# Latent features drawn between the blocks of a feed-forward, keys and values ahead of queries, and query loads on ScalarE's queue

## The chip, the cores and the metric

The kernel runs on one core of a Trainium2 chip. The metric is the device time of one execution in microseconds (us). TensorE (PE in the profile) does matmuls and transposes, VectorE (DVE) and ScalarE (ACT) read its results out of PSUM, GpSimd (POOL) does small vector work, and SyncE (SP) has a queue that starts DMAs. ScalarE has such a queue too: a DMA that it starts stands in its program among its own instructions. Each engine works through its instructions in their order.

## The reference, cut to what matters

Two layers over 1024 latent tokens and 256 context tokens of width 1024, all in float32. The first mixes with a short convolution and a gating unit, the second with attention; each ends in a feed-forward. The change touches the end of the first layer (the context's feed-forward) and the attention of the second.

```python
h_lat = _modulate(x, m_lat[0], m_lat[1]); h_ctx = _modulate(ctx, m_ctx[0], m_ctx[1])
q_l = _axial_rope(_proj_q(h_lat, w_q, q_g), tables)       # 8 heads of 128
k_l, v_l = _proj_kv(h_lat, w_kv, k_g)                     # 2 key and value heads
k_l = _axial_rope(k_l, tables)
k_c, v_c = _proj_kv(h_ctx, w_kv, k_g)                     # context: no rotation
k_all = jnp.concatenate([k_l, k_c], axis=1)
v_all = jnp.concatenate([v_l, v_c], axis=1)
y_lat = _attend(q_l, k_all, v_all) @ w_out                # softmax over 1280 keys
x = _post_norm(x, y_lat, m_lat[2], ln_g[l, 0], ln_b[l, 0])
```

`_proj_q` and `_proj_kv` multiply by the weights and normalise each head by its root mean square; `_modulate` is `h * (1 + scale) + shift`.

## The kernel before

Float32 products are made of three matmuls in a rounded format: each operand is split into a rounded half (hi) and a rest (lo), and `mm3` (lines 89 to 92) multiplies hi by hi, hi by lo and lo by hi. So each operand costs one ScalarE cast and one VectorE subtraction: `split` (L201, L202) for activations, `prep` for weights (load L80, cast L84, subtraction L86).

The latent tokens are eight tiles of 128 rows, in two groups g of four. `ln_spill` normalises a tile and stores it in `xn2_d`. `ln_mod` then makes the features of a group: in eight steps k, four 128x128 transposes on TensorE (L258), two ScalarE activations with scale and shift (L192, L195) and one VectorE subtraction (L198). The context has two tiles, so its steps have two transposes and 256 columns. The transposes go through PSUM buffers of the tag `tr`, of which there are two.

In the kernel before, this part of the program reads: spill and features of group 0, spill and features of group 1; the context's feed-forward `ffn` in blocks of two hidden tiles (weights prepared, gate and up products of 256 columns, SiLU at L470, products with the output weights); normalisation and features of the context; q projections (half 0, then half 1 of the heads, eight tiles each); keys and values of the context; keys and values of the latent groups 0 and 1. `tok_mm` makes a projected tile in 24 matmuls, `rms_rope` (L900 to L922) normalises and rotates it over ScalarE, VectorE and GpSimd, and transposes (L944 for q, L969 and L981 for keys) turn it. Queries of tiles 4 to 7 are stored in DRAM (`q_d`).

The attention goes through units of a tile, a key head and a pair of heads. `load_q` fetches `q_d` for tiles 4 to 7, two loads of 256 KB for each tile and key head, 16 in all. They are not let ahead of the normalisation (`norm`, L1041, GpSimd) of an earlier unit. The scores of a unit begin two units ahead of its use; the first matmuls that read a loaded q tile are those on the context's keys. `resid_bg` and `resid_store` load, scale and store the residual in the background (L1096, L1099, L1106), also on SyncE's queue.

A scheduler sets the order of instructions on each engine from its own model of time, within the data's dependences and the few ordering hints in the code.

Of the kernel before, what the change touches and what calls it, by code (L numbers as in the profile page):

```python
# [8 lines left out]
F32 = mybir.dt.float32  # L9
# [19 lines left out]
def hybrid_kernel(ctx: ExitStack, tc: tile.TileContext, A, out):  # L29
# [18 lines left out]
    def U(shape, dt):  # L48
        return up.tile(shape, dt, tag="u", name="u")
# [28 lines left out]
    def prep(src, gate=None, lo_eng=None):  # L78
        wf = wp.tile([P, 1024], F32, tag="wf", name="wf", bufs=WB[0])
        nc.sync.dma_start(out=wf, in_=src)  # L80
        if gate is not None:
            nc.vector.tensor_tensor(out=wf, in0=wf, in1=gate, op=ALU.mult)
        hi = wp.tile([P, 1024], F32R, tag="hi", name="hi", bufs=WB[1])
        nc.scalar.copy(hi, wf)  # L84
        lo = wp.tile([P, 1024], F32R, tag="lo", name="lo", bufs=WB[1])
        (lo_eng or nc.vector).tensor_tensor(out=lo, in0=wf, in1=hi.bitcast(F32), op=ALU.subtract)  # L86
        return hi, lo
# [74 lines left out]
    def step(n=1):  # L162
        for _ in range(n):
            next(bg)
# [7 lines left out]
    def mod_cols(v, l, sub, ln):  # L172
        sh, s1 = cols(v, l, 3 * sub), cols(v, l, 3 * sub + 1)
        g, b = lnc[:, ln[0], ln[1], 0, :], lnc[:, ln[0], ln[1], 1, :]
        s = const.tile([P, KD], F32, name=f"ms{v}{l}{sub}")
        o = const.tile([P, KD], F32, name=f"mo{v}{l}{sub}")
        nc.vector.tensor_scalar(out=s1, in0=s1, scalar1=1.0, scalar2=None, op0=ALU.add)
        nc.vector.tensor_tensor(out=s, in0=s1, in1=g, op=ALU.mult)
        nc.vector.tensor_tensor(out=o, in0=s1, in1=b, op=ALU.mult)
        nc.vector.tensor_tensor(out=o, in0=o, in1=sh, op=ALU.add)  # L180
        return s, o
# [18 lines left out]
    def split(src, hi, lo):  # L200
        nc.scalar.copy(hi, src)  # L201
        return nc.vector.tensor_tensor(out=lo, in0=src, in1=hi.bitcast(F32), op=ALU.subtract)  # L202
# [45 lines left out]
        while deferred:  # L248
            deferred.pop(0)()

    def ln_mod(pp, acc, so):

        n = len(acc) * P
        res = []
        for k in range(KD):
            ps = pp.tile([P, 512], F32, tag="tr", name="tr", bufs=2)
            for i, a in enumerate(acc):
                nc.tensor.transpose(ps[:, i * P:(i + 1) * P], a[k // 4][:, (k % 4) * P:(k % 4 + 1) * P], ident)  # L258
            if n == 512:
                hi, lo = U([P, 512], F32R), U([P, 512], F32R)  # L260
            else:
                t = U([P, 2, n], F32R)
                hi, lo = t[:, 0, :], t[:, 1, :]
            split_mod(ps[:, :n], so[0][:, k:k + 1], so[1][:, k:k + 1], hi, lo, True)
            res.append((hi, lo))
        return res

    def out_block(pp, acts, ws, acc, groups, xres=None, xscale=1.0):  # L270
# [184 lines left out]
        return last  # L455


    def ffn(pp, l, hT, v, acc, nb=2, steps=0, hook=None):
        groups = list(range(len(hT)))
        n = hT[0][0][0].shape[-1]  # L460
        gate = gate_bc(v, l, 5)

        def block_in(b):
            acts = {g: [] for g in groups}
            wg = [(prep(A["ffn_in"][l, j]), prep(A["ffn_in"][l, NJ + j])) for j in range(b * nb, b * nb + nb)]
            for g in groups:
                for w in wg:
                    pg = in_tile(pp, w[0], hT, g)
                    sg = T()
                    nc.scalar.activation(sg[:, :n], pg, AF.Silu)  # L470
                    pu = in_tile(pp, w[1], hT, g)
                    nc.vector.tensor_tensor(out=sg[:, :n], in0=pu, in1=sg[:, :n], op=ALU.mult)
                    hi, lo = act_pair(n)
                    marks["in"] = split(sg[:, :n], hi, lo)
                    acts[g].append((hi, lo))
            return acts

        pend = {g: [] for g in groups}
        j0 = 0

        def out(n):
            nonlocal pend, j0
            ws = [prep(A["ffn_out"][l, j0 + q], gate) for q in range(n)]
            out_block(pp, {g: pend[g][:n] for g in groups}, ws, acc, groups)
            pend = {g: pend[g][n:] for g in groups}
            j0 += n

        nblk = NJ // nb
        for b in range(nblk):
            cur = block_in(b)  # L490
            run_deferred()
            if b == nblk - 1:
                out(2 * nb - LASTK)
            elif b > 0:
                out(nb)
            pend = {g: pend[g] + cur[g] for g in groups}
            step(steps)
        if hook is not None:
            hook()
        out(LASTK)  # L500
# [218 lines left out]
    def ln_spill(a, t, xn):  # L719
        ln_norm(a)  # L720
        for h in range(2):
            nc.sync.dma_start(out=xn[t * P:(t + 1) * P, h * 512:(h + 1) * 512], in_=a[h])
# [144 lines left out]
    so = mod_cols(0, 1, 0, (0, 1))  # L867
    xr_d = dp.tile([SEQ, D], F32, name="xr_d")
    xn2_d = dp.tile([SEQ, D], F32, name="xn2_d")
    hT = []  # L870
    for g in range(2):
        for t in range(4 * g, 4 * g + 4):
            ln_spill(acc[t], t, xn2_d)
        hT.append(ln_mod(pp, [acc[t] for t in range(4 * g, 4 * g + 4)], so))


    hc = hcf
    ffn(pp, 0, hc, 1, accc)
    so = mod_cols(1, 1, 0, (0, 1))
    for t in range(2):  # L880
        ln_norm(accc[t])
    hc = [ln_mod(pp, [accc[0], accc[1]], so)]


    gqk = M2([P, 4, P])
# [2 lines left out]
    def tables(w, g):  # L888
        C, S = U([P, 4, P], F32), U([P, 4, P], F32)
        nc.sync.dma_start(out=C, in_=A["cosT"][:, 4 * g:4 * g + 4, :])  # L890
        nc.sync.dma_start(out=S, in_=A["sinT"][:, 4 * g:4 * g + 4, :])
        nc.gpsimd.tensor_tensor(out=C, in0=C, in1=gqk[:, 2 * w:2 * w + 1, :].to_broadcast([P, 4, P]), op=ALU.mult)
        nc.gpsimd.tensor_tensor(out=S, in0=S, in1=gqk[:, 2 * w + 1:2 * w + 2, :].to_broadcast([P, 4, P]), op=ALU.mult)
        return C, S
# [35 lines left out]
            mm3(ps, (a[0][:, c:c + P], a[1][:, c:c + P]), (ww[0][:, ks], ww[1][:, ks]), k == 0, k == KD - 1)  # L930
        return ps

    q_d = dp.tile([8, 2, 2, P, 512], F32, name="q_d")
    qT = {}
    qtab = [tables(0, 0), tables(0, 1)]
    for half in range(2):
        wq = [prep(A["wq"][half, i]) for i in range(4)]
        for t in range(8):
            g, i = divmod(t, 4)
            ps = tok_mm(hT[g], i * P, wq)  # L940
            q = rms_rope(ps, 4, qtab[g], i)
            tr = pp.tile([P, 512], F32, tag="tr", name="tr", bufs=2)
            for h in range(4):
                nc.tensor.transpose(tr[:, h * P:(h + 1) * P], q[:, h * P:(h + 1) * P], ident)  # L944
            hi, lo = U([P, 512], F32R), U([P, 512], F32R)
            split(tr, hi, lo)
            if g == 0:
                qT[t, half] = (hi, lo)
            else:
                nc.sync.dma_start(out=q_d[t, half, 0], in_=hi.bitcast(F32))  # L950
                nc.sync.dma_start(out=q_d[t, half, 1], in_=lo.bitcast(F32))

    wkv = [prep(A["wkv"][i]) for i in range(4)]
    kT, V = {}, []

    def kv_tile(hTg, c, tab, i):
        ps = tok_mm(hTg, c, wkv)
# [2 lines left out]
        split(ps[:, 256:512], v[:, 0, :], v[:, 1, :])  # L960
        return k, v

    Vc = []
    ktr = [pp.tile([P, 512], F32, tag="tr", name="tr", bufs=2) for _ in range(2)]
    for t in range(2):
        k, v = kv_tile(hc[0], t * P, None, 0)
        Vc.append(v)
        for kv in range(2):
            nc.tensor.transpose(ktr[kv][:, t * P:(t + 1) * P], k[:, kv * P:(kv + 1) * P], ident)  # L969
    for kv in range(2):  # L970
        c = U([P, 2, 256], F32R)
        split(ktr[kv][:, 0:256], c[:, 0, :], c[:, 1, :])
        kT[kv, 2] = (c[:, 0, :], c[:, 1, :])
    for g in range(2):
        ktab = tables(1, g)
        ktr = [pp.tile([P, 512], F32, tag="tr", name="tr", bufs=2) for _ in range(2)]
        for i in range(4):
            k, v = kv_tile(hT[g], i * P, ktab, i)
            V.append(v)
            for kv in range(2):  # L980
                nc.tensor.transpose(ktr[kv][:, i * P:(i + 1) * P], k[:, kv * P:(kv + 1) * P], ident)  # L981
        for kv in range(2):
            hi, lo = U([P, 512], F32R), U([P, 512], F32R)
            split(ktr[kv], hi, lo)
            kT[kv, g] = (hi, lo)
    V += Vc
    ppA.__exit__(None, None, None)
    wpA.__exit__(None, None, None)
# [14 lines left out]
    def load_q(n):  # L1003
        t, kv, p = units[n]
        if t >= 4 and p == 0:
            qT[t, kv] = (U([P, 512], F32R), U([P, 512], F32R))
            for x in range(2):
                i1 = nc.sync.dma_start(out=qT[t, kv][x].bitcast(F32), in_=q_d[t, kv, x])
                after(i1, [norm[2 * (n - 6)]])

    def score_a(n, h):
# [239 lines left out]
```

## Time and profile before

| | |
|---|---|
| median of 3 runs | 2629.03 us (2627.96 to 2629.47) |
| profiled execution | 2629.6 us, of which the span 2627.7 us |
| mean granted TensorE clock | 0.987 |
| busy: TensorE, VectorE, ScalarE, GpSimd | 97%, 70%, 36%, 12% |
| context's feed-forward | some 1137 to 1353 us |
| projections q, then keys and values | some 1353 to 1506 us |
| attention | some 1506 to 1834 us |

The span is the time from the first to the last instruction of the profiled execution. TensorE is the busiest engine by far. The page gives busy time over the whole span, and its chain of waits says which engine's work ended last; a timeline lists one engine's instructions in order of time with the idle time ahead of each and what ended it.

### The profile page before, as it was taken

The numbers are of one execution on the slowest core, as the hardware profiler recorded it, in microseconds if no ns is written. First come the engines' busy times: TensorE is split into PE (matmuls) and PEld (weight loads), VectorE is DVE, ScalarE is ACT, GpSimd is POOL, SyncE is SP. The second block draws the span as 40 slices with busy tenths as digits, with TensorE's granted clock in tenths as the row PEclk, the third lists the DMA queues.
The fourth block names the chain that finished last, engine by engine and source line by source line (L and its number), as shares of the span: only waits on it lengthen the run. The fifth ranks groups of instructions, "written<-read, shape, count | busy, mean of one in ns | idle before, by whom it ended". The sixth has DMA issues, their size and how long they took to land. (4 is left out here: it accounts for less than half of the span.)

```text
span 2627.7 us, 34744 instructions
## 1 busy us (share of the span) xinstructions
PE 2541.2 (97%) x12956; PEld 2138.1 (81%) x12956; DVE 1851.3 (70%) x3162; ACT 933.4 (36%) x1656; POOL 326.2 (12%) x254
## 2 busy tenths in 40 slices
PE   8999999999999999989999999999989999999997
PEld 6778888787788888879988789888868888888885
DVE  3888488999866655687759488777688665663267
ACT  1311145323233323164433277666163333342220
POOL 0132000112200020010006332222001000000001
PEclk9999999999999999989999999999999999999998
DMA  8453155344422753266541100113324222243232
GB/s 242 144 186 110 57 168 171 118 160 141 129 81 83 268 175 110 91 227 195 183 141 52 41 29 25 65 41 102 131 73 144 81 81 89 80 168 133 68 117 77
DMA packets 156106, 313.68 MB, mean 119 GB/s; under 512 B 25696, under 2 KB 45152, under 8 KB 155936
## 3 DMA queue, kind: packets, MB, share of 16 engines
q1 hardware_dynamic: 155936, 311.46, 36.1%
q8 instruction: 102, 1.67, 0.3%
q14 instruction: 68, 0.56, 0.1%
HBM read 262.05 MB, written 49.35 MB: 119 GB/s over the span
## 5 line engine op out<-in xcount | busy, mean ns | idle before, releaser
L90 PE MATMUL mm<-u,w 128*128 128x512 f32 x1232 | 480.6, 392 | 11.9 <-DVE m L591 4.5
L91 PE MATMUL mm<-u,w 128*128 128x512 f32 x1232 | 482.8, 392 | 3.8 <-DVE u L202 2.8
L92 PE MATMUL mm<-u,w 128*128 128x512 f32 x1232 | 476.7, 391 | 1.9 <-DVE w L202 1.9
L90 PE MATMUL mm<-w,u 128*128 128x512 f32 x832 | 322.7, 392 | 5.8 <-ACT u L201 3.0
L91 PE MATMUL mm<-w,u 128*128 128x512 f32 x832 | 324.3, 390 | 0.0
L92 PE MATMUL mm<-w,u 128*128 128x512 f32 x832 | 321.5, 390 | 0.0
L201 ACT CAST w<-sw 128x512 fp32r<-128x512 f32 x264 | 163.2, 622 | 419.7 <-PE mm L91 365.9
L202 DVE TENSOR_TENSOR w<-sw,w 128x512 fp32r<-128x512 f32 x264 | 191.1, 728 | 169.8 <-ACT w L201 138.5
L90 PEld LDWEIGHTS mm<-u,w 128*128 128x128 f32 x1232 | 232.8, 189 | 64.0 <-DVE m L591 6.4
L91 PEld LDWEIGHTS mm<-u,w 128*128 128x128 f32 x1232 | 232.7, 189 | 53.6 <-DVE u L202 4.6
L92 PEld LDWEIGHTS mm<-u,w 128*128 128x128 f32 x1232 | 232.8, 189 | 50.9 <-DVE w L202 2.6
L90 PE MATMUL mm<-u,hi 128*128 128x256 f32 (+1 forms) x736 | 238.5, 324 | 3.3 <-ACT tt L470 1.8
L84 ACT CAST hi<-wf 128x1024 fp32r<-128x1024 f32 x134 | 138.8, 1050 | 285.3 <-PE mm L91 76.9
L92 PE MATMUL mm<-u,lo 128*128 128x256 f32 (+1 forms) x736 | 237.5, 324 | 0.8 <-DVE lo L86 0.8
L91 PE MATMUL mm<-u,hi 128*128 128x256 f32 (+1 forms) x736 | 237.8, 323 | 0.0
L90 PE MATMUL mm<-hi,u 128*128 128x512 f32 x536 | 209.3, 395 | 3.6 <-DVE tt L917 1.3
L91 PE MATMUL mm<-lo,u 128*128 128x512 f32 x536 | 210.0, 392 | 2.1 <-DVE lo L86 2.1
L92 PE MATMUL mm<-hi,u 128*128 128x512 f32 x536 | 205.7, 393 | 0.0
L86 DVE TENSOR_TENSOR lo<-wf,hi 128x1024 fp32r<-128x1024 f32 x134 | 164.5, 1238 | 43.2 <-ACT hi L84 43.2
L90 PEld LDWEIGHTS mm<-w,u 128*128 128x128 f32 x832 | 157.2, 189 | 39.4 <-ACT u L201 3.9
L92 PEld LDWEIGHTS mm<-w,u 128*128 128x128 f32 x832 | 156.6, 188 | 32.7
L91 PEld LDWEIGHTS mm<-w,u 128*128 128x128 f32 x832 | 156.6, 188 | 32.3
(186 smaller groups left out, 4538.8 us busy)
## 6 DMA issues: line engine op xcount, KB each, us to landing
raw<-in_ffn_in SPq DMA_DIRECT2D x88, 512.0 KB
ad<-in_ada_w SPq DMA_DIRECT2D x112, 256.0 KB
act<-m SPq DMA_DIRECT2D x88, 256.0 KB
raw<-act SPq DMA_DIRECT2D x44, 512.0 KB
sw<-in_ffn_out SPq DMA_DIRECT2D x88, 256.0 KB
wf<-in_ffn_in SPq DMA_DIRECT2D x44, 512.0 KB
wf<-in_w_m SPq DMA_DIRECT2D x32, 512.0 KB
ab<-in_ada_w SPq DMA_DIRECT2D x48, 256.0 KB
```

The lines of the kernel that those rows point to most:

```text
L84: nc.scalar.copy(hi, wf)
L86: (lo_eng or nc.vector).tensor_tensor(out=lo, in0=wf, in1=hi.bitcast(F32), op=ALU.subtract)
L90: nc.tensor.matmul(ps, s[0], m[0], start=first, stop=False, skip_group_check=more)
L91: nc.tensor.matmul(ps, s[0], m[1], start=False, stop=False, skip_group_check=more)
L92: return nc.tensor.matmul(ps, s[1], m[0], start=False, stop=last, skip_group_check=more)
L201: nc.scalar.copy(hi, src)
L202: return nc.vector.tensor_tensor(out=lo, in0=src, in1=hi.bitcast(F32), op=ALU.subtract)
```

## The change

Three things change.

1. All eight latent tiles are spilled first. `ln_mod` becomes a generator, `ln_mod_k`, which stops after each of its steps; `ffn` gets an argument `each`, called at the end of every block, and takes two steps of the latent features there. Sixteen steps are thus asked for in blocks 0 to 7.
2. After the feed-forward the order is: keys and values of latent group 0, features of the context, keys and values of the context, those of latent group 1, then queries in the order (group 1, half 0), (group 1, half 1), (group 0, half 1), (group 0, half 0). The weights of half 0 are prepared twice, those of half 1 once.
3. The loads of q tiles are started from ScalarE's queue.

```diff
-    def ln_mod(pp, acc, so):
+    def ln_mod_k(pp, acc, so, res):
...
             split_mod(ps[:, :n], so[0][:, k:k + 1], so[1][:, k:k + 1], hi, lo, True)
             res.append((hi, lo))
+            yield
+
+    def ln_mod(pp, acc, so):
+        res = []
+        for _ in ln_mod_k(pp, acc, so, res):
+            pass
         return res
...
             step(steps)
+            if each is not None:
+                each(b)
...
-        hT.append(ln_mod(pp, [acc[t] for t in range(4 * g, 4 * g + 4)], so))
-    hc = hcf
-    ffn(pp, 0, hc, 1, accc)
+    for t in range(8):
+        ln_spill(acc[t], t, xn2_d)
+    def next_features(b):
+        for _ in range(2):
+            next(feats, None)
+    ffn(pp, 0, hcf, 1, accc, each=next_features)
+    for _ in feats:
+        pass
...
-    for half in range(2):
-        wq = [prep(A["wq"][half, i]) for i in range(4)]
-        for t in range(8):
...
+    kv_latent(0)
+    hc = [ln_mod(pp, [accc[0], accc[1]], soc)]
+    kv_context()
+    kv_latent(1)
...
+    for g, half in ((1, 0), (1, 1), (0, 1), (0, 0)):
+        if (g, half) in ((1, 0), (0, 1)):
+            qtab = tables(0, g)
+        if (g, half) != (0, 1):
+            wq = [prep(A["wq"][half, i]) for i in range(4)]
+        for i in range(4):
+            t = 4 * g + i
...
-                i1 = nc.sync.dma_start(out=qT[t, kv][x].bitcast(F32), in_=q_d[t, kv, x])
+                i1 = nc.scalar.dma_start(out=qT[t, kv][x].bitcast(F32), in_=q_d[t, kv, x])
                 after(i1, [norm[2 * (n - 6)]])
```

`kv_latent`, `kv_context` and the body of the query loop are the code of before, put into functions. In the changed file L257 is the feature transpose, L965 the latent keys' transpose, L1031 the q load.

The first place is the start of the context's feed-forward on TensorE; `tr<-ident,u` are feature transposes, `mm<-u,hi` and `mm<-u,lo` the first products. Before:

```order
L92 MATMUL mm<-w_9094,u 128x512
L258 MATMUL tr<-ident,u 128x128 x20
L90 MATMUL mm<-u,hi 128x256
L91 MATMUL mm<-u,hi 128x256
L92 MATMUL mm<-u,lo 128x256
L90 MATMUL mm<-u,hi 128x256
```

After:

```order
L92 MATMUL mm<-w_9094,u 128x512
L257 MATMUL tr<-ident,u 128x128 x8
L90 MATMUL mm<-u,hi 128x256
L91 MATMUL mm<-u,hi 128x256
L90 MATMUL mm<-u,hi 128x256
L91 MATMUL mm<-u,hi 128x256
L92 MATMUL mm<-u,lo 128x256
```

Twelve of the twenty transposes that stood ahead of the first product are gone from there, and the first two matmuls of a second product come ahead of the third of the first. The other transposes follow in eights between later blocks.

The second place is TensorE where the context's features are made; `tr_11864` and `tr_11872` before, `tr_12086` and `tr_12094` after, are their transposes of steps 0 and 1 (from `u_9272` and `u_9276`, the context's tiles), `mm_12065` before is a q product, `mm_12033` after the last product of `kv_latent(0)`, and `tr_11896`, `tr_11897` the keys' transposes. Before:

```order
L92 MATMUL mm_12065<-hi_11945,u_9586 128x512
L90 MATMUL mm_12065<-hi_11945,u_9596 128x512
L258 MATMUL tr_11864<-ident_75,u_9272 128x128
L258 MATMUL tr_11872<-ident_75,u_9272 128x128
L91 MATMUL mm_12065<-lo_11947,u_9596 128x512
L92 MATMUL mm_12065<-hi_11945,u_9597 128x512
L258 MATMUL tr_11864<-ident_75,u_9276 128x128
L258 MATMUL tr_11872<-ident_75,u_9276 128x128
L90 MATMUL mm_12065<-hi_11951,u_9607 128x512
```

After:

```order
L91 MATMUL mm_12033<-lo_11888,u_10418 128x512
L92 MATMUL mm_12033<-hi_11886,u_10419 128x512
L965 MATMUL tr_11896<-ident_75,tt_12020 128x128
L965 MATMUL tr_11897<-ident_75,tt_12020 128x128
L965 MATMUL tr_11896<-ident_75,tt_12065 128x128
L965 MATMUL tr_11897<-ident_75,tt_12065 128x128
L257 MATMUL tr_12086<-ident_75,u_9272 128x128
L257 MATMUL tr_12086<-ident_75,u_9276 128x128
L257 MATMUL tr_12094<-ident_75,u_9272 128x128
L257 MATMUL tr_12094<-ident_75,u_9276 128x128
L90 MATMUL mm_12152<-hi_11868,u_12089 128x512
```

Before, they lie between matmuls of a product already under way. Now they follow the transposes of the last two key tiles, with no matmul between, and the matmuls behind them (`mm_12152`, keys of the context) read their result.

The third place is the first load of a q tile: on SyncE before, where L1106 is the residual's store and L1096 its load:

```order
L1106 DMA xr_d_9526<-tt_14830 128x512
L1096 DMA tt_15063<-xn2_d_9527 128x512
L1106 DMA xr_d_9526<-tt_15063 128x512
L1008 DMA u_15256<-q_d_11930 128x512
L1008 DMA u_15257<-q_d_11930 128x512
L1096 DMA tt_15305<-xn2_d_9527 128x512
```

and on ScalarE after, where `ph` and `u` are casts of probabilities and of a unit's output:

```order
L201 CAST ph_15276<-tr_15271 128x512
L201 CAST u_15166<-tr_15190 128x256
L1031 DMA u_15280<-q_d_12434 128x512
L1031 DMA u_15281<-q_d_12434 128x512
L201 CAST ph_15307<-tr_15302 128x512
L201 CAST ph_15339<-tr_15334 128x512
```

TensorE after, with the last matmuls of that output (`tr_15190`) and the first that read the loaded `u_15280`:

```order
L90 MATMUL tr_15190<-ph_15257,u_12227 128x256
L91 MATMUL tr_15190<-u_15258,u_12227 128x256
L92 MATMUL tr_15190<-ph_15257,u_12227 128x256
L90 MATMUL tr_15286<-u_12232,u_15280 128x256
L91 MATMUL tr_15286<-u_12232,u_15280 128x256
L90 MATMUL sa_15285<-u_12078,u_15280 128x512
```

The loads have left SyncE's stores and now stand behind the cast of `tr_15190`, whose last matmul is the one just ahead of the first use. The same holds at four of the eight pairs; at two the instruction ahead is an exponential, at two a cast of probabilities (`ph`). The order of TensorE's rows here is that of before.

## Rows read from the trace of the kernel before

**Rows 1.** The page's first part: busy time, share of the span, instructions.
```profile
PE 2541.2 (97%) x12956; PEld 2138.1 (81%) x12956; DVE 1851.3 (70%) x3162; ACT 933.4 (36%) x1656; POOL 326.2 (12%) x254
```

**Rows 2.** Windows: length; PE, PEld, DVE, ACT, POOL busy (instructions); granted clock; DMA share; GB/s.
```profile
1138.00:1150.00 12.00, 8.40 (x52) 7.49 (x53) 9.72 (x16) 10.66 (x15) 1.47 (x2) 0.86 0.98 329
1166.00:1182.00 16.00, 9.63 (x50) 8.56 (x49) 14.63 (x22) 12.07 (x21) 0.00 (x0) 0.68 0.48 170
...
1200.00:1350.00 150.00, 150.00 (x1027) 140.01 (x1026) 118.31 (x146) 65.19 (x86) 0.00 (x0) 1.00 0.58 186
1385.00:1500.00 115.00, 115.00 (x546) 94.79 (x545) 80.11 (x213) 30.04 (x56) 55.21 (x51) 1.00 0.14 51
```

**Rows 3.** Timeline of TensorE, feed-forward's start: start, length, instructions [idle before <-releaser].
```profile
1136.84 1.04 PE L258 MATMUL tr<-ident,u 128*128 128x128 f32 x8
...
1167.53 0.65 PE L258 MATMUL tr<-ident,u 128*128 128x128 f32 x4 [1.25 <-ACT tt L195]
...
1175.06 0.58 PE L90 MATMUL mm<-u,hi 128*128 128x256 f32 x1 [1.84 <-ACT tt L470]
```

**Rows 4.** Timeline of ScalarE, the first two weight casts of the feed-forward.
```profile
1141.70 1.05 ACT L84 CAST hi<-wf 128x1024 fp32r<-128x1024 f32 x1
...
1144.09 1.04 ACT L84 CAST hi<-wf 128x1024 fp32r<-128x1024 f32 x1
```

**Rows 5.** Timeline of TensorE, the two waits in the projections.
```profile
1383.39 0.47 PE L90 MATMUL mm<-hi,u 128*128 128x512 f32 x1 [1.32 <-DVE tt L917]
...
1505.54 0.69 PE L981 MATMUL tr<-ident,tt 128*128 128x128 f32 x2 [3.10 <-DVE tt L922]
```

**Rows 6.** Groups by shape in the projections, GpSimd and VectorE: busy, mean ns.
```profile
L919 POOL TENSOR_TENSOR tt<-tt 128x512 f32<-128x512 f32 x16 | 22.4, 1402 | 4.4 <-DVE tt L917 2.1 <-ACT tt L900 1.3 <-PE tr L944 1.0
...
L919 POOL TENSOR_TENSOR tt<-tt 128x256 f32<-128x256 f32 x8 | 5.9, 738 | 3.1 <-DVE ms L903 3.1
...
L922 DVE TENSOR_TENSOR tt<-tt,rs 128x512 f32<-128x512 f32 x16 | 10.9, 683 | 5.5 <-POOL tt L919 5.5
...
L922 DVE TENSOR_TENSOR tt<-tt,rs 128x256 f32<-128x256 f32 x10 | 4.8, 476 | 2.5 <-POOL tt L919 1.4 <-POOL rs L905 0.9
```

**Rows 7.** Timeline of TensorE in the attention, four first uses of q tiles.
```profile
1650.02 0.28 PE L90 MATMUL tr<-u 128*128 128x256 f32 x1
...
1691.19 0.28 PE L90 MATMUL tr<-u 128*128 128x256 f32 x1
...
1711.05 0.28 PE L90 MATMUL tr<-u 128*128 128x256 f32 x1
...
1733.71 0.36 PE L90 MATMUL tr<-u 128*128 128x256 f32 x1 [3.40 <-DMA u<-q_d]
```

**Rows 8.** Windows in the attention and at its end, columns as in rows 2.
```profile
1640.00:1800.00 160.00, 149.63 (x1040) 135.51 (x1039) 122.25 (x263) 105.67 (x247) 42.15 (x31) 0.99 0.18 60
...
1734.30:1737.50 3.20, 3.20 (x16) 3.00 (x15) 0.69 (x1) 0.59 (x1) 0.00 (x0) 0.50 0.08 26
1756.00:1760.00 4.00, 3.72 (x25) 3.35 (x26) 0.88 (x3) 1.27 (x3) 1.34 (x1) 1.00 0.26 97
1833.30:1839.90 6.60, 5.78 (x13) 4.46 (x14) 6.14 (x10) 3.42 (x6) 0.00 (x0) 0.50 0.80 262
```

**Rows 9.** Timeline of ScalarE around three of these first uses.
```profile
1650.55 0.38 ACT L201 CAST u<-tr 128x256 fp32r<-128x256 f32 x1
...
1689.13 1.06 ACT L201 CAST ph<-tr 128x512 fp32r<-128x512 f32 x2
...
1711.05 0.52 ACT L1033 ACTIVATE pt<-pt,nm 128x256 f32<-128x256 f32 x1
```

**Rows 10.** Timeline of SyncE's queue, the pair of loads that came latest.
```profile
1730.95 0.88 SPq L1008 DMA_DIRECT2D u<-q_d  x2
```

**Rows 11.** Waits of SyncE's queue from 1600 to 1800: us in total, times, longest.
```profile
SPq L1106 <- DVE rc L1040: 89.7, 5, 20.3
```

**Rows 12.** Who waited for the q loads of line 1008: us, times.
```profile
  PE tr L90: 4.8, 2
```

More of the change, by code (lines that the diff above doesn't have):

```diff
@@ L249, in run_deferred @@
             deferred.pop(0)()
-    def ln_mod(pp, acc, so):
+    def ln_mod_k(pp, acc, so, res):
         n = len(acc) * P
-        res = []
         for k in range(KD):
@@ L455, in mixer, with ffn @@
         return last
-    def ffn(pp, l, hT, v, acc, nb=2, steps=0, hook=None):
+    def ffn(pp, l, hT, v, acc, nb=2, steps=0, hook=None, each=None):
         groups = list(range(len(hT)))
@@ L869, in hybrid_kernel, with to_features @@
     xn2_d = dp.tile([SEQ, D], F32, name="xn2_d")
[L870 to L873, printed above, removed]
-        hT.append(ln_mod(pp, [acc[t] for t in range(4 * g, 4 * g + 4)], so))
-    hc = hcf
-    ffn(pp, 0, hc, 1, accc)
-    so = mod_cols(1, 1, 0, (0, 1))
+    hT = [[], []]
+    def to_features():
+        for g in range(2):
+            yield from ln_mod_k(pp, [acc[t] for t in range(4 * g, 4 * g + 4)], so, hT[g])
+    feats = to_features()
+    for t in range(8):
[6 more added lines that the diff above has]
+        pass
+    soc = mod_cols(1, 1, 0, (0, 1))
     for t in range(2):
         ln_norm(accc[t])
-    hc = [ln_mod(pp, [accc[0], accc[1]], so)]
+    hc = [[]]
     gqk = M2([P, 4, P])
@@ L931, in tok_mm @@
         return ps
-    q_d = dp.tile([8, 2, 2, P, 512], F32, name="q_d")
-    qT = {}
-    qtab = [tables(0, 0), tables(0, 1)]
-    for half in range(2):
-        wq = [prep(A["wq"][half, i]) for i in range(4)]
-        for t in range(8):
[L939 to L951, printed above, removed]
     wkv = [prep(A["wkv"][i]) for i in range(4)]
-    kT, V = {}, []
+    kT, V, Vc = {}, [], []
     def kv_tile(hTg, c, tab, i):
@@ L961, in kv_tile, with kv_latent @@
         return k, v
[L963 to L974, printed above, removed]
+    def kv_latent(g):
         ktab = tables(1, g)
@@ L985, in hybrid_kernel, with kv_context @@
             kT[kv, g] = (hi, lo)
+    def kv_context():
+        ktr = [pp.tile([P, 512], F32, tag="tr", name="tr", bufs=2) for _ in range(2)]
+        for t in range(2):
+            k, v = kv_tile(hc[0], t * P, None, 0)
+            Vc.append(v)
+            for kv in range(2):
+                nc.tensor.transpose(ktr[kv][:, t * P:(t + 1) * P], k[:, kv * P:(kv + 1) * P], ident)
+        for kv in range(2):
+            c = U([P, 2, 256], F32R)
+            split(ktr[kv][:, 0:256], c[:, 0, :], c[:, 1, :])
+            kT[kv, 2] = (c[:, 0, :], c[:, 1, :])
+    kv_latent(0)
+    hc = [ln_mod(pp, [accc[0], accc[1]], soc)]
+    kv_context()
+    kv_latent(1)
+    q_d = dp.tile([8, 2, 2, P, 512], F32, name="q_d")
+    qT = {}
+    for g, half in ((1, 0), (1, 1), (0, 1), (0, 0)):
[5 more added lines that the diff above has]
+            t = 4 * g + i
+            ps = tok_mm(hT[g], i * P, wq)
+            q = rms_rope(ps, 4, qtab, i)
+            tr = pp.tile([P, 512], F32, tag="tr", name="tr", bufs=2)
+            for h in range(4):
+                nc.tensor.transpose(tr[:, h * P:(h + 1) * P], q[:, h * P:(h + 1) * P], ident)
+            hi, lo = U([P, 512], F32R), U([P, 512], F32R)
+            split(tr, hi, lo)
+            if g == 0:
+                qT[t, half] = (hi, lo)
+            else:
+                nc.sync.dma_start(out=q_d[t, half, 0], in_=hi.bitcast(F32))
+                nc.sync.dma_start(out=q_d[t, half, 1], in_=lo.bitcast(F32))
     V += Vc
```

## The prediction

> **What bounds the kernel now.** I read the page's first part, then TensorE's idle time in order of time, then each place that the change touches. TensorE is busy 2541.2 of 2627.7 us [rows 1]: some 86 us of idle time and a little half-clock time are all that an unchanged set of matmuls can give back, and any wait put in front of TensorE is paid nearly in full. Four places matter. The start of the context's feed-forward has two holes, 8.40 busy us of 12 and 9.63 of 16 [rows 2], made mostly of waits for features (1.25 and 1.84 us among them [rows 3]) and for the first weights. From 1200 to 1350 TensorE has no gap at all [rows 2]. Two holes lie in the projections: 1.32 us and, at their end, 3.10 us [rows 5]. In the attention TensorE idles 160.0 - 149.6 = 10.4 us of 160 [rows 8]. 4.8 us of these are two waits for a q tile [rows 12], the longer one 3.40 us [rows 7]; the other six first uses waited for nothing, as at 1650.02. After the 3.40 us the granted clock was 0.50, the lower level (1.2 of 2.4 GHz), for 3.2 us; around 1833, where the attention ends, for 6.6 us; after the shorter of the two waits it stayed 1.00 [rows 8]. At half clock half of TensorE's busy time is lost, 1.6 us in those 3.2.
>
> **A, features between the feed-forward's blocks.** Removed: the two holes, 3.6 + 6.4 = 10.0 us of idle time, and their half clock. That is 12 x (1 - 0.86) = 1.7 us in the first and 16 x (1 - 0.68) = 5.1 us in the second, of which I put 1.5 on idle time counted already: 1.7 + 3.6 = 5.3. Six of the transpose groups there stand alone at 0.65 us; eight transposes in one go took 1.04, 0.52 a group [rows 3]: 6 x 0.13 = 0.8. Sum 16.1 us. What takes its place: after eight transposes, done at 1136.84 + 1.04 = 1137.88, the first matmul needs the first weight's rounded half. That cast ran from 1141.70 for 1.05 us, when the weight had come; the second weight's began at 1144.09 and took 1.04 [rows 4], so the matmuls can go on at 1142.8 and, after two of them, at 1145.2. SyncE's order is the same up to these loads, so they come no earlier. 4.9 and 1.9 us are idle, 6.8 together, and half clock for 3 to 6.6 us costs 1.6 to 3.3; I take 2.4. That is 9.2, and A = 9.2 - 16.1 = **-6.9** (-9 to -4.5, by the clock and by how much of the second wait other matmuls fill). The steps themselves fall into blocks 0 to 7: fourteen of the sixteen, with 28 activations and 14 VectorE operations. At the mean of the second hole (12.07 us for 21, 14.63 for 22) that is 16 us on ScalarE and 9 on VectorE, and from 1200 to 1350 these are free for 85 and 32 us [rows 2]: nothing. Without that cover each step would cost what it costs now, 0.65 + 1.25 = 1.9 us.
>
> **D, the wait at 1383.** The 1.32 us [rows 5] stood behind the context's activations on ScalarE, which leave this place: **-1.3**.
>
> **The first half's query weights are prepared twice:** four more 1.05 us casts, four subtractions, 2 MB of loads. From 1385 to 1500 TensorE is 100% busy, ScalarE has 85 us free, VectorE 35, and the DMA engines are busy 0.14 [rows 2]: nothing.
>
> **B, the handover inside keys and values.** Before, the context's transposes stood between q matmuls. Now kv_latent(0) ends, in TensorE's order, with the transposes of its last two key tiles right behind the last matmul, and right behind those come the context's first feature transposes. The last tile must first pass its norm and rotation: the 3.10 us at 1505.54 [rows 5] are the same chain, for the same two heads, with nothing behind it to fill. The context's transposes then need the keys' two PSUM buffers, each free only after a cast and a subtraction of 128x512, some 0.65 each (0.68 for a VectorE operation of that shape [rows 6]): 1.3 us. An activation, 0.6, follows before the first matmul. Idle 5.0 us, half clock 1.6 to 3.3, take 2.4: **+7.4** (from +3.1, buffers free and the clock kept, to +8.3).
>
> **C, the end of the projections.** It is q tiles of four heads that end it now. Their chain has two steps on GpSimd and three on VectorE of twice the columns; one of each is 1.40 against 0.74 and 0.68 against 0.48 us [rows 6]. I count the others like them: 2 x 0.66 + 3 x 0.20 = 1.9 us on top of the same 3.10, and up to 1.7 us of clock, take 0.6: **+2.5** (1.3 to 3.6).
>
> **E, the q loads on ScalarE's queue.** This is the main term. On SyncE each pair stands behind a store that waits for VectorE (five such waits alone sum to 89.7 us [rows 11]) and still came in time for six tiles of eight. On ScalarE each pair stands behind work that itself waits for TensorE just before the tile's first use, and TensorE's order there is unchanged. In four tiles that is the cast of an output that TensorE ends one matmul ahead: it began at 1650.55 for a use at 1650.02 [rows 7, 9]. From issue to first matmul one load took 1733.71 - 1730.95 = 2.76 us [rows 7, 10]. Stall: 0.53 + 2.76 = 3.3 us. In two tiles it is an exponential that runs from 1711.05 for 0.52 us, with the use at 1711.05 too: 3.3 again. In two it is the second of two casts that began together at 1689.13, so at about 1689.7, for a use at 1691.19: 1.3 to 1.7, take 1.5. Sum 6 x 3.3 + 2 x 1.5 = 22.8, less today's 4.8: +18.0. Six long stalls instead of one halve the clock five times more, 5 x 1.6 = +8.0. Against that, a stall lets VectorE and ScalarE catch up, so the other 10.4 - 4.8 = 5.6 us of idle time can vanish; I take all of it off. E = **+20.4**. Low end: no clock loss, +12.4. High end: nothing caught up, and the issue waits for the end of the cast before it (6 x 0.4): +28.4. This trace has no load issued by ScalarE; the price is SyncE's.
>
> In the trace a load waits for whatever stands before it on the queue that issues it [rows 11], so what decides is its place in that queue. The Trainium skill, page "Trainium Kernel Development and Optimization", section Key Constraints, says that DMAs from SyncE's, ScalarE's and GpSimd's queues run on the same DMA engines, and that issuing from several only saves issue time: by that alone E would be about nil.
>
> **Sum.** -6.9 - 1.3 + 7.4 + 2.5 + 20.4 = +22.1 on the profiled execution's 2629.6 us (span 2627.7): 2651.7. The median of the runs is 0.6 lower: 2651.1, say 2651.
>
> **Rivals.**
> (1) Not slower: ScalarE reaches its loads early. If the instruction ahead of each pair is released more than 2.8 us before the use, all q waits go, -4.8 and 1.6 of clock; E is -6.4, the sum -4.7, the time 2624.3. For it: ScalarE is busy only 105.7 of 160 us [rows 8]. Against it: what holds ScalarE there is TensorE's result, not its own load.
> (2) The queue is worth only issue time: E is 0, the sum +1.7, 2630.7. For it: six tiles of eight had slack. Against it: at 1730.95 the load was issued 0.6 us after TensorE could have used it (1733.71 - 3.40 = 1730.31) and the stall was paid in full; a place in the queue costs as much as it delays.
> (3) The handover is worse: the context's eight feature steps run one after the other with 1.25 us of wait each, as at 1167.53, without latent matmuls to fill: +10, 2661. Against it: by the order, blocks of latent matmuls stand behind the first two steps.
> (4) The stalls come but the clock holds, as after the shorter wait: E 12.4, 2643.
>
> **How the numbers follow.** Forecast with its bounds, (4) among them: 0.70; (1) 0.12, (2) 0.08, (3) 0.10. The low ends together (-9 - 1.3 + 3.1 + 1.3 + 12.4) give +6.5, 2635.5; the high ends (-4.5 - 1.3 + 8.3 + 3.6 + 28.4) +34.5, 2663.5, and (3) reaches there with a little more. The range 2635 to 2666 leaves out (1) and (2), 0.20. 0.2%, some 5.3 us, is about what a measurement of this kernel can tell from no change: (1) lies near that bound and gives half its chance to each side, (2) is no change, the rest is slower.
>
> **What would show it.** Right: in the changed profile TensorE waits before eight first uses of q tiles, six of them for over 3 us, with a load as the releaser and a granted clock of 0.50 behind them; the holes at the feed-forward's start are one of some 5 and one of some 2 us; a new wait of 4 to 5 us stands behind the last keys of kv_latent(0). Wrong: first uses without a wait, or loads issued long before them, take E away and with it the sign.

## The result: 18 us slower

| | before | changed |
|---|---|---|
| median (lowest to highest, 4 runs each) | 2628.49 us (2627.11 to 2629.47) | 2646.38 us (2645.87 to 2647.49) |
| ratio, 95% interval | | 1.0069 [1.0052, 1.0086] |
| span of the profiled execution | 2627.7 us | 2645.7 us |

The change makes the kernel 0.7% slower; 2651 was forecast, with 2635 to 2666 as the range. First the page of the changed kernel: the first part, which answers to [rows 1], and the groups of its chain of waits.

```profile
PE 2545.1 (96%) x12956; PEld 2142.1 (81%) x12956; DVE 1855.6 (70%) x3166; ACT 936.6 (35%) x1660; POOL 326.1 (12%) x254
...
PE mm L90 9%; PE mm L91 9%; PE mm L92 9%; PE tr L1070 2%; PE tr L91 1%; PE tr L90 1%; ACT pt L1055 1%; PE tr L92 1%; PE sa L90 1%; PE sa L91 1%; PE sa L92 1%; DMA u<-q_d 1%; DVE u L202 1%; ACT ph L201 1%; DVE mx L1051 0%
```

TensorE's busy time rose by 4 us at the same instruction count, its idle time by 14. `DMA u<-q_d`, the q loads, now has 1% of the chain.

Where it went is read best by stages that begin and end at corresponding matmuls in both kernels and hold the same number of them: the start of the context's feed-forward, the first projection, the first score, and a matmul some 2,390 further on, behind the attention. The windows (columns as in rows 2) of the kernel before:

```profile
1136.84:1347.34 210.50, 200.41 (x1385) 187.56 (x1384) 169.48 (x216) 108.67 (x148) 6.47 (x7) 0.97 0.63 204
1347.34:1505.88 158.54, 154.11 (x725) 126.48 (x724) 99.36 (x258) 41.83 (x79) 64.56 (x60) 1.00 0.16 55
1505.88:1885.58 379.70, 362.56 (x2392) 326.37 (x2391) 288.93 (x591) 233.50 (x534) 86.82 (x64) 0.98 0.19 63
1885.58:2599.60 714.02, 701.47 (x3101) 577.26 (x3100) 435.18 (x704) 218.43 (x366) 18.69 (x18) 0.99 0.30 100
```

and of the changed kernel:

```profile
1137.47:1341.32 203.85, 196.50 (x1385) 184.99 (x1384) 169.85 (x216) 107.91 (x148) 10.37 (x9) 0.97 0.65 214
1341.32:1507.69 166.37, 156.50 (x725) 128.07 (x724) 104.57 (x263) 46.53 (x84) 61.30 (x58) 0.97 0.18 62
1507.69:1903.67 395.98, 367.64 (x2392) 331.21 (x2391) 288.45 (x590) 233.04 (x533) 86.98 (x64) 0.97 0.18 60
1903.67:2617.67 714.00, 701.65 (x3101) 577.46 (x3100) 434.25 (x704) 218.13 (x366) 17.41 (x18) 0.99 0.30 100
```

The differences are -6.65 us in the feed-forward, +7.83 in the projections, +16.28 in the attention and nothing behind it. With 0.6 us ahead of the first that is the 18.0 us between the spans. These are two single executions, and a stage moves by some 3 us from one execution to the next: in runs described below, the feed-forward in its old form took 207.62 us in place of 210.50 (e2), and the attention with its loads on SyncE's queue 376.79 and 376.04 us in place of 379.70 (e3, e1).

TensorE's timeline of the changed kernel, first around the feed-forward and the projections, where [rows 3] and [rows 5] stood:

```profile
1137.47 1.04 PE L257 MATMUL tr<-ident,u 128*128 128x128 f32 x8
1145.12 0.58 PE L90 MATMUL mm<-u,hi 128*128 128x256 f32 x1 [6.61 <-ACT hi L84]
...
1146.65 0.58 PE L90 MATMUL mm<-u,hi 128*128 128x256 f32 x1 [0.73 <-ACT hi L84]
...
1367.14 0.69 PE L965 MATMUL tr<-ident,tt 128*128 128x128 f32 x2 [3.17 <-DVE tt L937]
...
1369.02 1.29 PE L257 MATMUL tr<-ident,u 128*128 128x128 f32 x4 [1.19 <-DVE u L202]
...
1506.95 1.09 PE L1001 MATMUL tr<-ident,tt 128*128 128x128 f32 x4 [5.45 <-DVE tt L937]
```

The first two waits replace the nine of the two holes before. 3.17 and 1.19 are the handover inside the keys and values, 5.45 the end of the projections with four heads; the 1.32 us wait of [rows 5] is gone. Then the attention, all waits for q loads, where [rows 7] stood:

```profile
1655.37 0.35 PE L90 MATMUL tr<-u 128*128 128x256 f32 x1 [2.94 <-DMA u<-q_d]
...
1679.12 0.36 PE L90 MATMUL tr<-u 128*128 128x256 f32 x1 [2.81 <-DMA u<-q_d]
...
1723.44 0.36 PE L90 MATMUL tr<-u 128*128 128x256 f32 x1 [1.13 <-DMA u<-q_d]
...
1746.34 0.55 PE L90 MATMUL tr<-u 128*128 128x256 f32 x1 [3.69 <-DMA u<-q_d]
...
1770.54 0.36 PE L90 MATMUL tr<-u 128*128 128x256 f32 x1 [2.13 <-DMA u<-q_d]
...
1793.73 0.36 PE L90 MATMUL tr<-u 128*128 128x256 f32 x1 [2.78 <-DMA u<-q_d]
...
1817.09 0.55 PE L90 MATMUL tr<-u 128*128 128x256 f32 x1 [1.38 <-DMA u<-q_d]
```

Seven waits, 16.9 us, where there were two with 4.8 [rows 12]. Windows behind three of them and over the stretch of [rows 8]:

```profile
1723.50:1726.70 3.20, 3.20 (x22) 2.89 (x23) 1.20 (x4) 0.76 (x2) 1.34 (x1) 1.00 0.50 164
1793.80:1797.00 3.20, 3.20 (x23) 2.94 (x24) 0.78 (x2) 1.25 (x3) 0.00 (x0) 1.00 0.02 6
1746.40:1749.60 3.20, 3.20 (x13) 2.90 (x14) 0.13 (x1) 0.59 (x1) 0.00 (x0) 0.50 0.28 106
1640.00:1800.00 160.00, 141.01 (x952) 128.10 (x951) 112.62 (x238) 94.94 (x220) 37.53 (x28) 0.96 0.16 50
```

The clock was halved behind the 3.69 us wait and held behind the 1.13 and the 2.78. It was halved behind the 2.94 and the 2.81 as well, and behind the 1.38 (0.50 from 1816.90 to 1819.90), and held behind the 2.13 (1.00 from 1770.60 to 1773.80). Over the 160 us of [rows 8] TensorE was busy for 141.0 us, where it had been 149.6.

Why the waits are shorter than forecast is seen on ScalarE. Its timeline and its queue (ACTq, the rows in which a load is issued) around the second pair of loads and around the fourth:

```profile
1675.95 0.58 ACT L201 CAST ph<-tr 128x512 fp32r<-128x512 f32 x1
1676.35 0.33 ACTq L1031 DMA_DIRECT2D u<-q_d  x1
1676.42 0.39 ACT L201 CAST u<-tr 128x256 fp32r<-128x256 f32 x1
...
1720.54 0.33 ACTq L1031 DMA_DIRECT2D u<-q_d  x1
...
1721.04 1.14 ACT L1055 ACTIVATE pt<-sa,nm 128x1024 f32<-128x1024 f32 x1
...
1722.14 0.52 ACT L1056 ACTIVATE pt<-pt,nm 128x256 f32<-128x256 f32 x1
```

In the program the second pair stands behind the cast at 1676.42 and the fourth behind the exponential at 1722.14. They are issued before these begin, by 0.07 and by 1.6 us: the queue does not wait until the instruction ahead runs. It does wait for what the instructions ahead wait for: TensorE's last matmul before the second pair ended at 1679.12 - 2.81 = 1676.31, 0.04 us ahead of the issue, and at the other three pairs behind such a cast the issue came 0.04 to 0.10 us behind TensorE's last matmul. Ahead of the fourth pair stands, two instructions further up, a cast that waits for TensorE's transposes:

```profile
1719.45 1.04 PE L1070 MATMUL tr<-ident,pt 128*128 128x128 f32 x8
```

They ended at 1720.49, 0.05 us ahead of that issue.

### The profile page after: what moved, and what is told of

Read it like the earlier page. It is cut to its first block, busy times and chain, and to the rows that moved or that the text cites. A ratio compares the mean times of both kernels' runs of the same rounds, so it can differ in the third digit from the quotient of the medians.

```text
span 2645.7 us, 34734 instructions
## 1 busy us (share of the span) xinstructions
PE 2545.1 (96%) x12956; PEld 2142.1 (81%) x12956; DVE 1855.6 (70%) x3166; ACT 936.6 (35%) x1660; POOL 326.1 (12%) x254
## 5 line engine op out<-in xcount | busy, mean ns | idle before, releaser
L86 DVE TENSOR_TENSOR lo<-wf,hi 128x1024 fp32r<-128x1024 f32 x138 | 170.1, 1244 | 47.0 <-ACT hi L84 46.6
```

## Experiments

The theory after the result: the place of the loads in ScalarE's program makes the attention some 15 us longer; features between the blocks gain 6 to 7; the new order costs about 8 in the projections. Rivals: the new order slows the attention whatever the queue; ScalarE's queue is slow in itself; the feed-forward's gain is given back later. Medians and intervals are against runs of the kernel before on the same chip (medians 2626.62, 2626.30 and 2626.85 us for the three groups).

**Loads back on SyncE (e1).** The changed kernel with

```diff
-                i1 = nc.scalar.dma_start(out=qT[t, kv][x].bitcast(F32), in_=q_d[t, kv, x])
+                i1 = nc.sync.dma_start(out=qT[t, kv][x].bitcast(F32), in_=q_d[t, kv, x])
```

> The changed kernel with the q loads back on SyncE's queue. Theory (the loads' place in ScalarE's program makes the attention longer by 15.4 us; the rest of the change nets about +2): the time falls by 15 to 2631 us, 1.5 to 3 us above the kernel before; TensorE waits some 5 us or less for q loads. Rival (the new order of keys, values and queries makes the attention slower, whatever the queue): it stays near 2646 and TensorE still waits about 17 us for q loads.

Measured 2627.05 us, ratio 1.0000 [0.9991, 1.0009]. What the feed-forward gains, the projections lose: without the third part the change is worth nothing. The fall is 19 us, where 15 was expected. The attention's stage:

```profile
1508.97:1885.01 376.04, 360.41 (x2393) 325.29 (x2392) 287.13 (x589) 233.04 (x533) 86.72 (x64) 0.99 0.19 63
```

**Only the queue (e2).** The kernel before with the opposite edit.

> The kernel before with nothing changed but the queue of the q loads, ScalarE's in place of SyncE's. Theory: +15, about 2644 us, with waits of 1 to 4 us ahead of seven or eight first uses, some 17 us in all. Rival (the waits come with the new order): 2628 to 2631 us.

Measured 2646.9 us, ratio 1.0081 [1.0068, 1.0093]: the whole loss, and a little more, from one word. The attention's stage took 396.25 us, against 395.98 in the changed kernel. Its window, with that of the feed-forward, which is the one of before here:

```profile
1139.93:1347.55 207.62, 199.09 (x1385) 186.69 (x1384) 169.34 (x216) 108.46 (x148) 6.59 (x7) 0.98 0.63 207
1506.07:1902.32 396.25, 365.63 (x2393) 331.01 (x2391) 288.61 (x590) 233.47 (x534) 87.00 (x64) 0.97 0.18 60
```

Who waited for the q loads, in e1 and in e2 (us, times):

```profile
  PE tr L90: 4.3, 2
```

```profile
  PE tr L90: 20.4, 8
```

The rival of the new order falls. In e2's program six of the eight pairs stand behind the cast of an output; TensorE waited 2.77 to 3.34 us for each of these, and 1.59 and 1.04 us for the other two.

**Only the features (e3).** The kernel before with part 1.

```diff
-    ffn(pp, 0, hc, 1, accc)
+    for t in range(8):
+        ln_spill(acc[t], t, xn2_d)
+    ffn(pp, 0, hcf, 1, accc, each=next_features)
```

> The kernel before with part 1 alone: all spills first, latent features drawn between the feed-forward's blocks. Theory (part 1 is worth what the changed kernel gained up to the first projection): -6.7, about 2622 us. Rival (the gain is given back later, since the context's normalisation or the first projections come to wait): 2626 us or more.

Measured 2621.17 us, ratio 0.9986 [0.9978, 0.9995]: 5.5 us faster by the medians (1.3 to 5.8 by the interval). The feed-forward's stage took 202.65 us and the projections 158.46, as before the change; the gain isn't given back.

```profile
1135.76:1338.41 202.65, 196.37 (x1385) 184.85 (x1384) 169.91 (x216) 107.96 (x148) 7.91 (x7) 0.98 0.64 212
1338.41:1496.87 158.46, 154.03 (x726) 126.48 (x724) 99.45 (x258) 41.84 (x79) 64.56 (x60) 1.00 0.16 55
1496.87:1873.66 376.79, 359.94 (x2392) 324.27 (x2391) 288.87 (x590) 233.49 (x534) 86.80 (x64) 0.99 0.19 63
```

**The loads a unit earlier, still on ScalarE's queue (e4).** The changed kernel with

```diff
         if i == 0:
-            load_q(n)
             score_a(n, 0)
+            if n + 1 < N:
+                load_q(n + 1)
```

> The changed kernel, loads still on ScalarE's queue, but asked for one unit earlier, so that some 40 matmuls lie between the instruction ahead of a load and its first use in TensorE's order. Theory (place in the program decides): all q waits and the half clock behind them go, 2646 - 16.9 - 4 to 5 = 2624 to 2626 us. Rival (a load by ScalarE's queue is slow in itself or holds ScalarE up): 2640 us or more.

Measured 2616.19 us, ratio 0.9966 [0.9953, 0.9978]. All q waits of the matmuls are gone, with the same sixteen loads on the same queue; the rival of a slow queue falls. But the time is some 8 us under what was expected: the attention is shorter by more than the waits cost.

```profile
1506.99:1871.81 364.82, 356.52 (x2392) 324.34 (x2391) 288.20 (x589) 231.95 (x533) 86.95 (x64) 0.99 0.20 65
```

364.8 us against 376.0 in e1. The q waits of e1 were 4.3 us, with one stretch of half clock behind them (1.7 us); some 5 us remain. The scheduler laid out the rest of each unit differently too, with fewer short waits on ScalarE and VectorE: over the attention, eleven with 4.8 us in all where e1 has eighteen with 8.1 (one of 2.8 us at its end, in both, left out). Which of that is due to the lead and which to the order wasn't separated.

**Early loads, features, old order (e5), the fastest; and the same on SyncE (e6).** e3 with the edit of e4 on ScalarE's queue, and on SyncE's.

> The kernel before with part 1 (features between the feed-forward's blocks) and the q loads on ScalarE's queue one unit earlier; keys, values and queries in the order of before. Theory (part 1 gains 6 to 8, early loads make the attention some 11 to 15 us shorter than before, the new order is the part that costs): 16 to 19 us under the kernel before, so 6 to 9 under the run that had early loads and the new order. Rival (the new order costs nothing by itself): no more than 11 under before.

> The same as the run before it in this list, but the loads, asked for one unit earlier, on SyncE's queue. Theory (what counts is how early the queue reaches the load; an early load on SyncE still stands behind a store that waits for VectorE, but has a unit more): within 3 us of that run. Rival (ScalarE's queue is better in itself, or SyncE's stores still hold loads up): 5 us or more slower, with waits for q loads of 4 us or more in all.

e5 measured 2605.93 us, ratio 0.9927 [0.9915, 0.9939], faster than both kernels; e6 2607.34 us, 0.9932 [0.9919, 0.9944]. No matmul waits for a q load in either. Once the load is asked for early, the queue makes no difference that these runs show. The stages of e5:

```profile
1135.81:1337.64 201.83, 195.98 (x1386) 184.46 (x1384) 169.94 (x216) 107.82 (x148) 7.31 (x7) 0.98 0.63 213
1337.64:1496.12 158.48, 154.05 (x726) 126.47 (x724) 99.35 (x258) 41.77 (x79) 64.50 (x60) 1.00 0.16 55
1496.12:1859.25 363.13, 354.91 (x2392) 323.41 (x2391) 289.16 (x590) 232.20 (x534) 86.73 (x64) 0.99 0.20 65
```

Against e4, where they took 166.58 us, the projections are 8.1 us shorter: that is the price of the new order.

**How much lead is needed (e9).** e5, but the next unit's load is asked for after `score_a(n, 1)`, half a unit later:

```diff
         if i == 0:
             score_a(n, 0)
-            if n + 1 < N:
-                load_q(n + 1)
...
         elif i == 2:
             score_a(n, 1)
+            if n + 1 < N:
+                load_q(n + 1)
```

> As the fastest kernel so far (features between the blocks, order of before, loads on ScalarE's queue), but the loads are asked for half a unit ahead instead of a whole one: some 22 matmuls, about 3 us, lie between the work ahead of a load and its first use. Theory (a load takes 2.4 to 2.6 us on its own and 3.1 to 3.7 beside the residual's DMAs; only what is not covered is paid): waits of up to 0.7 us at some of the eight uses, under 3 us in all, attention 364 to 368 us, 2606 to 2611 us. Rival (the gain of the early loads is not the lead but the order that the scheduler makes around a load a whole unit ahead): the waits go and the attention still takes 370 us or more.

Measured 2607.20 us, ratio 0.9928 [0.9914, 0.9941], attention 364.24 us. Who waited for the loads, on TensorE:

```profile
  PE tr L90: 1.7, 4
  PE sa L90: 0.3, 1
```

Half a unit of lead covers the load but for 0.4 us or so at four uses and 0.3 at a fifth. The attention keeps the whole gain (363.13 us in e5), so the rival, that the gain hangs on the order made around a load a whole unit ahead, falls.

**Stores after the weights (e7).** e5, with the tiles normalised ahead of the feed-forward and stored in its blocks:

```diff
     for t in range(8):
-        ln_spill(acc[t], t, xn2_d)
+        ln_norm(acc[t])
...
             next(feats, None)
+        if b < 8:
+            for h in range(2):
+                nc.sync.dma_start(out=xn2_d[b * P:(b + 1) * P, h * 512:(h + 1) * 512], in_=acc[b][h])
```

> As the first of this list, but the latent tiles are only normalised ahead of the feed-forward, and each is stored after one of its blocks, so that SyncE's queue reaches the first weights without sixteen stores of normalised tiles among them. Theory (the 5 to 6.6 us hole in front of the feed-forward is the first weight's late load, behind these stores): the hole shrinks to 2 to 4 us and the time falls by 2 to 4 us. Rival (the weights wait for their buffers or for the feed-forward's gate instead): the hole and the time stay within 1 us.

Measured 2605.78 us, ratio 0.9923 [0.9909, 0.9936], and a hole of 5.49 us: no gain. The scheduler put several stores back ahead of the weights, so the edit did only part of what it says: four weights were issued in a row, but the first no earlier than in e5 (1136.03 us against 1135.57). SyncE's queue, ScalarE's casts and the window of the hole:

```profile
1136.03 2.25 SPq L80 DMA_DIRECT2D wf<-in_ffn_in  x4
```

```profile
1142.67 1.04 ACT L84 CAST hi<-wf 128x1024 fp32r<-128x1024 f32 x1 [5.61 <-DMA wf<-in_ffn_in]
1143.95 1.04 ACT L84 CAST hi<-wf 128x1024 fp32r<-128x1024 f32 x1 [0.23 <-DMA wf<-in_ffn_in]
1145.28 1.05 ACT L84 CAST hi<-wf 128x1024 fp32r<-128x1024 f32 x1 [0.28 <-DMA wf<-in_ffn_in]
```

```profile
1138.00:1150.00 12.00, 6.04 (x33) 5.51 (x32) 8.52 (x14) 4.56 (x5) 2.39 (x2) 0.72 1.04 361
```

The casts follow each other by 1.3 us, one weight of 512 KB each, while the DMA engines are busy all the time (0.98 before, too [rows 2]). The first weight's cast began 6.6 us after its issue; before it had been 5.1 (1136.61 to 1141.70). So the theory, that the hole is these stores ahead of the first weight, was not put to the test: the first weight's place behind stores did not change. That the loads' own rate makes part of the hole fits these rows and isn't shown; a run that thins out the other traffic there wasn't made.

**The handover covered (e8).** e4, with the context's features drawn between the tiles of the second query pass and its keys made after that pass.

```diff
     kv_latent(0)
-    hc = [ln_mod(pp, [accc[0], accc[1]], soc)]
-    kv_context()
     kv_latent(1)
+    ctx_feats = ln_mod_k(pp, [accc[0], accc[1]], soc, hc[0])
...
+            if (g, half) == (1, 1):
+                for _ in range(2):
+                    next(ctx_feats, None)
```

> The changed kernel with early loads (new order of keys and values first), but the context's features are drawn between q tiles of a later pass, and its keys and values made after that pass, so that the handover from the first to the second latent group has matmuls to run. Theory (the wait behind the last key tiles, 3.2 + 1.2 us, and the half clock behind it are the handover's price): 5 to 7 us faster than the run with early loads and the new order, so 15 to 17 us under before, and the 5.4 us wait at the end of the projections stays. Rival (these waits are moved, not removed): within 2 us of that run, 9 to 12 under before.

Measured 2624.82 us, ratio 0.9992 [0.9983, 1.0001]: 8.6 us slower than e4, where 5 to 7 faster was expected. A miss. The two waits at the handover are gone, and more have come elsewhere in the projections (three of TensorE's waits; the first two kinds occur three times each; then the stage's window):

```profile
1444.75 0.50 PE L90 MATMUL mm<-hi,u 128*128 128x512 f32 x1 [0.93 <-ACT u L192]
...
1450.03 0.47 PE L90 MATMUL mm<-hi,u 128*128 128x512 f32 x1 [1.55 <-DVE tt L932]
...
1514.06 1.09 PE L1007 MATMUL tr<-ident,tt 128*128 128x128 f32 x4 [3.81 <-DVE tt L937]
```

```profile
1340.94:1516.65 175.71, 158.66 (x725) 126.59 (x724) 104.80 (x263) 46.46 (x84) 63.62 (x58) 0.99 0.17 59
```

The stage takes 175.7 us against 166.6 in e4. So the price of the new order isn't a single wait that can be filled from any side; the order before, with the context's features between q matmuls and a two-headed end, was the cheaper of the three.

## Why the prediction held, step by step

- **A, feed-forward.** -6.9 was worked out, -6.65 measured by the two profiled executions. The parts came out too: TensorE's idle time in the stage fell by 2.7 us, where 3.2 was put, and its busy time by 3.9, where 3.7 was. The agreement is closer than the measurement can tell: e3 gives -5.5 by the medians, -5.8 to -1.3 by the interval. Within the idle time the waits are 6.61 + 0.73 = 7.3 us in place of 4.9 + 1.9 = 6.8: the first weight's cast ended at 1145.1, not 1142.8, since its load was issued at 1138.9, 2.3 us later than before, behind stores of normalised tiles. The cover held: no wait for a latent feature is left in the stage.
- **B, C and D, projections.** Together +8.6 worked out, +7.83 measured. The handover waits 3.17 + 1.19 = 4.4 us, where 5.0 was put, and TensorE's busy time in the stage rose by 2.4 us, as put for its clock; no further wait shows behind the second. The end waits 5.45 us, where 3.10 + 1.9 = 5.0 was put; the half clock behind it falls into the next stage. D went as said. The four weights prepared twice cost no visible wait.
- **E, the q loads.** +20.4 was worked out. The stages of the two profiled executions give +16.3, with about 1 us of C's clock in it; e2, whose edit is this part alone, gives +20.3 by the medians (17.9 to 24.4 by the interval). Most of the gap is that the attention before was in its profile some 3 us longer than in e1 and e3, whose loads are on SyncE's queue too. So the total holds, but in part by luck: in the changed kernel's profile each of its three parts is smaller than put, and two of them add while the third takes off.
  - The stalls: 16.9 us in place of 22.8. Behind the casts of outputs they were 2.94, 2.81, 3.69 and 2.78 (3.3 was put), behind the exponentials 1.13 and 2.13 (3.3 was put), behind the two other casts 0 and 1.38 (1.5 was put). Of eight first uses seven waited, and one for over 3 us, where six had been named as the sign. The step that failed is when a load is issued: the prediction dated the issue by when the instruction ahead begins or, at the exponentials, by when it ends. The rows of ScalarE's queue above show it issued ahead of both, as soon as what the instructions ahead wait for has come. At the exponentials the issue came 1.6 and 1.35 us before they began, and these two stalls make 3.3 of the 5.9 us that were put too much.
  - The clock: TensorE's busy time in the attention rose by 367.64 - 362.56 = 5.1 us, not 8.0; not every stall of nearly 3 us brought it down.
  - The catching up: 5.6 us of other waits were taken off, but of the attention's 17.1 us idle before, 12.3 weren't q waits, and 28.3 - 16.9 = 11.4 remain: 0.9 vanished.
- **The rivals.** (1) asked for an issue 2.8 us ahead of use, which e4 then made on purpose: it came out 10 us under the kernel before, not 5, since an early load gained more than the waits it took away. (2), only issue time, falls with e2. (3) did not come: behind the handover's second wait there is no further one. (4), stalls with the clock held, is what happened at three of seven waits (1.13, 2.13 and 2.78 us).

The Trainium skill, page "Trainium Kernel Development and Optimization", section Key Constraints, says that DMAs of the three queues share the same engines and that issuing from several only saves issue time. e5 and e6 agree where loads are early (2605.93 and 2607.34 us); e2 shows what it leaves open, 20 us for the place behind which a load waits. The Trainium skill's page "DMA: Bandwidth & Descriptors", section "Anatomy of one DMA — SWDGE (gpsimd) path", says that a semaphore wait happens on the issuing sequencer and that DMA engines do not wait; it speaks of GpSimd's path, and the issue at 1676.35, right after TensorE's matmul, agrees with it for ScalarE's.

## What to carry to other kernels

Moving a load to another engine's queue moves it behind that engine's waits: look at what stands ahead of it there and when that is released, against first use less the load's time (here some 2.8 us). If a load comes late, ask for it earlier before choosing a queue: half a unit of lead on ScalarE's queue, or a unit on SyncE's, was worth some 14 us here against e3. A rearrangement that fills one hole should be timed by stage, since here it gained 6.7 us in one stage and paid 7.8 in the next, and in more than one execution, since a stage moved by 3 us between two.

## What the runs showed of the hardware that I had not expected

- ScalarE's queue issued a DMA up to 1.6 us before the instruction that stands ahead of it in ScalarE's program began (1720.54 against 1722.14).
- The clock was not a function of the length of the one wait before it: 1.00 behind waits of 2.78 and 2.13 us, 0.50 behind 3.69 and also behind 1.38.
- Where four weights were asked for in a row (e7), the first one's cast began 6.6 us after its issue, against 5.1 before, where two were; the DMA engines were busy throughout in both (1.04 and 0.98). That the one makes the other isn't shown.
